# Four engines in a written order: scan and output projection of layer 0 as one software pipeline

## The chip, the cores and the metric

The kernel runs on one core of a Trainium2 chip. A core has five engines that issue independently, each from its own queue in order: TensorE (PE in the profile, its weight loads PEld), VectorE (DVE), ScalarE (ACT), GpSimd (POOL) and SyncE (SP), which here only issues DMAs. The metric is the device time of one execution in microseconds; less is better.

## The reference

Two layers of a hybrid trunk are computed for 128 context tokens and 1024 latent tokens of width 1024. Layer 0 runs windowed attention and a bidirectional state-space scan side by side behind one input projection and adds a joint output projection to the residual. Layer 1 is latent attention. The part that matters is the scan of layer 0, in chunks of 128 tokens for 16 heads of 64, once per direction, and what follows it:

```python
diff = cum[:, :, :, None, :] - cum[:, :, None, :, :]
decay = jnp.exp(jnp.where(causal, diff, -jnp.inf))
scores = jnp.einsum("bclhn,bcshn->bclsh", ch, bh) * decay
y_diag = jnp.einsum("bclsh,bcshp->bclhp", scores, xd)
...
y_off = jnp.einsum("bclhn,bchpn,bclh->bclhp", ch, h_in, jnp.exp(cum))
...
y = y_f + flip(y_b) + d_skip[:, None] * xs
...
s_out = rms_norm(y.reshape(b, L, SSD_INNER) * jax.nn.silu(z), gnorm_w)
return jnp.concatenate([a_out, s_out], axis=-1) @ w_out
...
xl = xl + gate * out
```

The next layer begins with `rms_norm(xl) * (1 + scale) + shift`.

## The kernel before

The work of this stage is cut into nine tiles of 128 tokens: latent tiles 0 to 7 and the context tile, number 8 (`NLT`). Each tile passes two functions.

`scan_out(p, sp, c)` takes the chunk's inputs from DRAM scratch: `BC` (the scan's B and C, transposed), `xs`, `zs` (the SiLU gate), `H` (incoming states, both directions stacked on the partitions). `Gp` is the product of B and C for both head groups (L973), copied to `G` by ScalarE (L975). GpSimd starts `y` with the skip term (L985). For each of two groups of eight heads: two state products on TensorE (`off`, L992), scaled on VectorE (L994) and added into `y` on GpSimd (L995); then two blocks of four heads each. A block loads the cumulated log decays of its heads, broadcast to all partitions, into `cu` (L1000, 512 KB); GpSimd masks each direction (L1003); ScalarE takes the exponentials, eight of 128x128 (L1005); VectorE adds the two directions and multiplies with `G` (L1007, L1008); TensorE multiplies with `xs` into `yacc` (L1011; the profile counts eight instructions for the four products). After both blocks VectorE adds `yacc` to `y` and multiplies with `zs` (L1012, L1013). At the end of the chunk ScalarE squares and sums (L1015), GpSimd computes the reciprocal root (`rstd_of`, L391 and L392), VectorE scales `y` (L1017), TensorE transposes it in two times four steps (L1022), and `split` cuts the result into a high and a low part: a cast on ScalarE (L249) and a subtraction on VectorE (L250).

`project_out` multiplies a tile with the output weights. A product in three parts (`mm3`, L256 to L258) runs over twelve blocks of 128 rows (four from attention, `at`, eight from the scan, `sT`) and two halves of 512 columns, so 72 matmuls of 512 columns per tile. The attention operands come from `project_operands` (a load, and `split`). `residual` multiplies a half with the gate on VectorE (L1060) and adds it to `x` on GpSimd (L1061). Then come a square (L1094), the reciprocal root, a scale (L1096), transposes (L1049), two modulations on VectorE (L1052, L1053) and the store of the next layer's input.

Buffers are rings: `cu`, `zs`, `xs`, `Hc`, `y`, `BC`, `G`, `x` and `rt` have two buffers, `xn` and `nf` one. PSUM has two buffers under each of the tags `pre`, `o`, `tr` and `mm`.

The order within an engine is made by a planner. It runs the program as written against its own model of time and issues on each engine what that model has ready first, earlier lines having priority. The order it finds is fixed when the program is built; on the chip each engine follows its list, and semaphores carry the dependences. `keep_in_program_order` pins an instruction behind the one written before it on its engine; a helper of layer 1, `pinned`, uses it for a few instructions. Chunks 8 and 0 of the scan are written earlier, woven into the stage before (`first_outputs`); the loop then writes, for each tile, the scan of that tile and the projection of the tile before it:

```python
for c in [NLT] + list(range(NLT)) + [None]:
    if c is not None:
        sT = sTs[c] if c in sTs else scan_out(p, op5, c)
    if prev is not None:
        ...
        project_out(p, op5, prev[0], prev[1], gate, start_latents if c is None else None)
```

`start_latents`, called in the middle of the last projection, frees half of the output weights and loads the first weights of layer 1.

Of the kernel before, what the change touches and what calls it, by code (L numbers as in the profile page):

```python
# [214 lines left out]

def bcast_rows(ap, n):
    return ap.unsqueeze(0).broadcast_to([n] + list(ap.shape))
# [3 lines left out]
def hybrid_trunk(ctx: ExitStack, tc: tile.TileContext, I, O, dbg=None, stage=99):  # L221
    nc = tc.nc
    pe, act, dve, pool, dma = nc.tensor, nc.scalar, nc.vector, nc.gpsimd, nc.sync
# [740 lines left out]

    def scan_out(p, sp, c):
        tok = slice(c * 128, (c + 1) * 128)
        BC = p.tile([128, 2, 2, 128], F32, tag="BC", name="BC", bufs=2)
        for d in range(2):
            dma.dma_start(BC[d * 64:(d + 1) * 64, 1], bc_d[1, :, tok].rearrange("(g n) t -> n g t", g=2))
        dma.dma_start(BC[0:64, 0], bc_d[0, :, tok].rearrange("(g n) t -> n g t", g=2))  # L970
        Gp = psum("pre", "Gp")
        for g in range(2):
            pe.matmul(Gp[:, g * 128:(g + 1) * 128], BC[0:64, 0, g], BC[0:64, 1, g], start=True, stop=True)  # L973
        G = p.tile([128, 2, 128], F32, tag="G", name="G", bufs=2)
        act.copy(G, Gp[:, 0:256].rearrange("p (g n) -> p g n", g=2))  # L975
        xs = p.tile([128, D], F32, tag="xs", name="xs", bufs=2)
        dma.dma_start(xs, xs_d[tok])
        zs = p.tile([128, D], F32, tag="zs", name="zs", bufs=2)
        dma.dma_start(zs, z_d[tok])
        if c < NLT:  # L980
            H = p.tile([128, D], F32, tag="Hc", name="Hc", bufs=2)
            dma.dma_start(H[0:64], H_d[c, 0:64])
            dma.dma_start(H[64:128], H_d[NLT - 1 - c, 64:128])
        y = p.tile([128, D], F32, tag="y", name="y", bufs=2)
        pool.tensor_tensor(heads(y), heads(xs), dskip.unsqueeze(2).broadcast_to([128, 16, 64]), ALU.mult)  # L985
        for g in range(2):
            cs = slice(g * 512, (g + 1) * 512)
            if c < NLT:
                for d in range(2):
                    off = psum("pre", "off")  # L990
                    ds = slice(d * 64, (d + 1) * 64)
                    pe.matmul(off, BC[ds, 1, g], H[ds, cs], start=True, stop=True)  # L992
                    t = p.tile([128, 512], F32, tag="rt", name="off", bufs=2)
                    dve.tensor_tensor(heads(t), heads(off), ex[:, d, c * 16 + g * 8:c * 16 + g * 8 + 8].unsqueeze(2).broadcast_to([128, 8, 64]), ALU.mult)  # L994
                    pool.tensor_tensor(y[:, cs], y[:, cs], t, ALU.add)  # L995
            acc = psum("o" if c < NLT else "pre", "yacc")
            for u in range(2):
                h0 = c * 16 + g * 8 + u * 4
                cu = p.tile([128, 4, 2, 128], F32, tag="cu", name="cu", bufs=2)
                dma.dma_start(cu, bcast_rows(cum_d[h0:h0 + 4], 128))  # L1000
                for d in range(2):
                    s = 1 - 2 * d
                    pool.affine_select(cu[:, :, d], cu[:, :, d], [[0, 4], [s, 128]], ALU.is_ge, NEG, base=0, channel_multiplier=-s)  # L1003
                    for j in range(4):
                        act.activation(cu[:, j, d], cu[:, j, d], AF.Exp, bias=nb[:, d, h0 + j:h0 + j + 1])  # L1005
                m = cu[:, :, 0]
                dve.tensor_tensor(m, m, cu[:, :, 1], ALU.add)  # L1007
                dve.tensor_tensor(m, m, G[:, g].unsqueeze(1).broadcast_to([128, 4, 128]), ALU.mult)  # L1008
                for j in range(4):
                    hc = (u * 4 + j) * 64  # L1010
                    pe.matmul(acc[:, hc:hc + 64], m[:, j], xs[:, g * 512 + hc:g * 512 + hc + 64], start=(u == 0 and j == 0), stop=(u == 1 and j == 3))  # L1011
            dve.tensor_tensor(y[:, cs], acc, y[:, cs], ALU.add)  # L1012
            dve.tensor_tensor(y[:, cs], y[:, cs], zs[:, cs], ALU.mult)  # L1013
        ssq = p.tile([128, 1], F32, tag="ssq", name="ssq", bufs=4)
        act.activation(zs, y, AF.Square, accum_out=ssq)  # L1015
        r = rstd_of(p, ssq, D, 1)
        dve.tensor_scalar(y, y, r, None, ALU.mult)  # L1017
        sT = sp.tile([128, 2, KT, 128], F32R, tag="sT", name="sT", bufs=2)
        for q in range(2):
            pt = psum("tr", "pt")  # L1020
            for j in range(4):
                pe.transpose(pt[:, j * 128:(j + 1) * 128], y[:, (q * 4 + j) * 128:(q * 4 + j + 1) * 128], ident)  # L1022
            split(sT[:, 0, q * 4:q * 4 + 4], sT[:, 1, q * 4:q * 4 + 4], pt.rearrange("p (k n) -> p k n", k=4))
        return sT
# [5 lines left out]
    def first_outputs():  # L1030
        for c in (NLT, 0):
            sTs[c] = scan_out(p5, op5, c)
            yield
# [9 lines left out]

    def norm_T(p, l, cond, xh, tok):

        for q in range(2):
            pt = psum("tr", "pt")
            for j in range(4):
                pe.transpose(pt[:, j * 128:(j + 1) * 128], xh[:, (q * 4 + j) * 128:(q * 4 + j + 1) * 128], ident)  # L1049
            full = p.tile([128, 4, 128], F32, tag="nf", name="nf", bufs=1)  # L1050
            bc = lambda v: v[:, l, q * 4:q * 4 + 4, cond].unsqueeze(2).broadcast_to([128, 4, 128])
            dve.tensor_tensor(full, pt.rearrange("p (k n) -> p k n", k=4), bc(scl), ALU.mult)  # L1052
            dve.tensor_tensor(full, full, bc(shift), ALU.add)  # L1053
            dma.dma_start(h1_d[q * 4:q * 4 + 4, :, tok].rearrange("k p n -> p k n"), full)
# [23 lines left out]
    def project_out(p, sp, t, sT, gate, beside=None):  # L1078
        tok = slice(t * 128, (t + 1) * 128)
        at = operands5.pop(t) if t in operands5 else project_operands(p, sp, t)  # L1080
        x = p.tile([128, D], F32, tag="x", name="x", bufs=2)
        dma.dma_start(x, I["x_sample"][0, tok] if t < NLT else I["x_prompt"][0])
        for q in range(2):
            acc = psum("mm", "acc")
            for k in range(12):
                h, l = (at[:, 0, k], at[:, 1, k]) if k < 4 else (sT[:, 0, k - 4], sT[:, 1, k - 4])
                mm3(acc, h, l, *wos[k, q], k == 0, k == 11)
            residual(p, q, acc, x, gate)
            if q == 0 and beside:
                beside()  # L1090
        dma.dma_start(x1_d[tok], x)
        ssq = p.tile([128, 1], F32, tag="ssq", name="ssq", bufs=4)
        xn = p.tile([128, D], F32, tag="xn", name="xn", bufs=1)
        act.activation(xn, x, AF.Square, accum_out=ssq)  # L1094
# [601 lines left out]
```

## Time and profile before

| | |
|---|---|
| median of 3 runs | 1854.38 us (1854.11 to 1855.22) |
| profiled execution | 1849.66 us, its span 1847.8 us |
| busy in the span: PE, PEld | 1713.8 us (93%), 1315.1 us (71%) |
| busy: DVE, ACT, POOL | 1045.4 us (57%), 817.2 us (44%), 744.2 us (40%) |
| mean granted TensorE clock | 0.958 |

Busy time of PE is modelled: a matmul's end includes its way through the array, so rows of matmuls in sequence overlap, and the distance between their starts is what each costs. Rows of time give start, length, engine, line, operation, operands, count and, in brackets, the idle time before it with what ended it. The nine projections of the stage lie between about 704 and 958 us of the span.

### The profile page before, as it was taken

The page shows a single profiled execution, that of the slowest core. Times are in us where ns is not written, and L with a number is a line of the kernel's source. Part 1 is how long each engine was busy: PE and PEld are TensorE (multiplying, and loading weights), DVE is VectorE, ACT ScalarE, POOL GpSimd, SP SyncE. Part 2 cuts the span into 40 slices and gives each one's busy share as a digit, 9 for nine tenths or more (in the row PEclk, how much of TensorE's full clock was granted, in tenths as well). Part 3 has the DMA queues.
Part 4 walks back from the last instruction along what each step waited for, and adds up shares of the span by engine and source line. Part 5 has one row for each costly group of instructions (what it writes and reads, how often), then busy time and mean ns, then how long its engine had stood idle before and what let it go on. Part 6 is the DMA issues. An engine that isn't in the chain of part 4 may idle for free.

```text
span 1847.8 us, 27078 instructions
## 1 busy us (share of the span) xinstructions
PE 1713.8 (93%) x9031; PEld 1315.1 (71%) x9031; DVE 1045.4 (57%) x1989; ACT 817.2 (44%) x1873; POOL 744.2 (40%) x741
## 2 busy tenths in 40 slices
PE   6899999999998878998899999999999998998898
PEld 3799999877775766666688898655665665654486
DVE  4665545655546467777665434655665664564243
ACT  4532323665655354444444322444545544545321
POOL 3510000133343345665623010466666665565432
PEclk9999999999999888999999999899999998999899
DMA  7423423434435697565463532020120121104342
GB/s 260 125 81 93 121 62 111 131 101 132 115 105 146 195 284 240 166 208 159 167 180 85 165 110 79 11 61 23 52 71 23 45 75 28 37 29 122 109 154 91
DMA packets 210655, 210.26 MB, mean 114 GB/s; under 512 B 36162, under 2 KB 175504, under 8 KB 210516
## 3 DMA queue, kind: packets, MB, share of 16 engines
q1 hardware_dynamic: 210372, 208.40, 37.8%
q8 instruction: 72, 1.18, 0.3%
q14 instruction: 67, 0.55, 0.1%
q0 software_dynamic: 144, 0.13, 0.0%
HBM read 151.94 MB, written 51.72 MB: 110 GB/s over the span
## 4 chain that ended last, share of the span: by engine, by line
PE 65%; DMA 11%; DVE 8%; POOL 4%; ACT 3%; issue 3%; SPq 2%; POOLq 0%; DVEq 0%; ACTq 0%
PE acc L256 12%; PE acc L258 12%; PE acc L257 12%; PE acco L1469 6%; PE sc L1448 3%; PE pp L1427 3%; PE sc L1450 3%; PE sc L1449 3%; DMA arenaG<-cum_d 2%; DVE arenaR L250 2%; DMA arenaF<-rd_d 2%; DMA rd_d<-arenaF 2%; PE st L808 1%; DVE arenaF L209 1%; POOL arenaG L1003 1%
## 5 line engine op out<-in xcount | busy, mean ns | idle before, releaser
L256 PE MATMUL acc<-arenaR 128*128 128x384 f32 (+4 forms) x1248 | 426.7, 343 | 20.0 <-ACT arenaR L249 8.0
L1484 POOL TENSOR_TENSOR arenaG<-arenaG 128x512 f32<-128x512 f32 x256 | 332.6, 1318 | 233.8 <-ACT arenaG L1455 201.1
L257 PE MATMUL acc<-arenaR 128*128 128x384 f32 (+3 forms) x1176 | 398.2, 339 | 0.1
L258 PE MATMUL acc<-arenaR 128*128 128x384 f32 (+4 forms) x1152 | 385.9, 336 | 0.2
L256 PEld LDWEIGHTS acc<-arenaR 128*128 128x128 f32 x1248 | 240.0, 193 | 61.7 <-issue 16.0
L1455 ACT ACTIVATE arenaG<-sc 128x512 f32<-128x512 f32 (+1 forms) x304 | 174.7, 580 | 224.2 <-PE sc L1450 206.7
L209 DVE TENSOR_REDUCE arenaF<-pp 128x1 f32<-128x384 f32 (+1 forms) x400 | 198.8, 539 | 102.2 <-PE pp L1427 100.2
L257 PEld LDWEIGHTS acc<-arenaR 128*128 128x128 f32 x1176 | 226.4, 193 | 15.7 <-issue 3.6
L258 PEld LDWEIGHTS acc<-arenaR 128*128 128x128 f32 x1152 | 221.6, 192 | 16.5 <-DVE arenaR L250 2.3
L250 DVE TENSOR_TENSOR arenaR<-arenaF,arenaR 128x512 fp32r<-128x512 f32 (+2 forms) x144 | 133.2, 938 | 73.3 <-ACT arenaR L249 68.5
L249 ACT CAST arenaR<-arenaF 128x512 fp32r<-128x512 f32 (+3 forms) x160 | 101.0, 649 | 138.9 <-issue 22.6
L1469 PE MATMUL acco<-arenaG 128*64 128x512 f32 (+1 forms) x608 | 152.0, 612 | 0.0
L1005 ACT ACTIVATE arenaG<-arenaG,arenaF 128x128 f32<-128x128 f32 x288 | 88.4, 389 | 113.0 <-POOL arenaG L1003 112.7
L1427 PE MATMUL pp<-arenaR 96*128 96x384 f32 (+1 forms) x300 | 97.6, 387 | 12.8 <-DVE arenaF L209 12.5
L749 POOL TENSOR_TENSOR arenaG<-arenaF,arenaG 128x512 fp32r<-128x512 f32 x28 | 47.8, 1708 | 150.8 <-PE acco L753 87.0
L1448 PE MATMUL sc<-arenaR 96*128 96x512 f32 (+1 forms) x228 | 94.9, 416 | 5.6 <-ACT arenaG L1455 5.4
L1427 PEld LDWEIGHTS pp<-arenaR 96*128 96x128 f32 x300 | 58.6, 203 | 57.3 <-DVE arenaF L209 28.4
L1450 PE MATMUL sc<-arenaR 97*128 97x512 f32 (+1 forms) x228 | 90.6, 400 | 1.0 <-DMA arenaR<-arenaF 1.0
L258 PE MATMUL acc<-arenaR,arenaS 128*128 128x512 f32 (+1 forms) x240 | 90.6, 382 | 0.0
L1449 PE MATMUL sc<-arenaR 96*128 96x512 f32 (+1 forms) x228 | 89.9, 394 | 0.0
L1469 PEld LDWEIGHTS acco<-arenaG 128*64 128x64 f32 x608 | 37.3, 141 | 71.4 <-issue 68.3
L1003 POOL TENSOR_SCALAR_AFFINE_SELECT arenaG<-arenaG 128x512 f32<-128x512 f32 x72 | 60.2, 859 | 63.3 <-DMA arenaG<-cum_d 56.4
(328 smaller groups left out, 3331.9 us busy)
## 6 DMA issues: line engine op xcount, KB each, us to landing
arenaF<-in_ada_w_dram SPq DMA_DIRECT2D x96, 256.0 KB
arenaG<-cum_d SPq DMA_DIRECT2D x36, 512.0 KB
arenaF<-in_ab_w_in_dram SPq DMA_DIRECT2D x51, 256.0 KB
z_d<-arenaF SPq DMA_DIRECT2D x36, 128.0 KB
xs_d<-arenaF SPq DMA_DIRECT2D x8, 576.0 KB
arenaF<-xs_d SPq DMA_DIRECT2D x9, 512.0 KB
arenaF<-z_d SPq DMA_DIRECT2D x9, 512.0 KB
x_d<-arenaG SPq DMA_DIRECT2D x9, 512.0 KB
```

The source lines that it names most:

```text
L209: f()
L250: lo_eng.tensor_tensor(lo, src, hi.bitcast(F32), ALU.subtract)
L256: pe.matmul(out, ah, bh, start=first, stop=False)
L257: pe.matmul(out, ah, bl, start=False, stop=False)
L258: pe.matmul(out, al, bh, start=False, stop=last)
L1427: pe.matmul(pp[:, 0:w], AQ[s][0:96, t * 128:(t + 1) * 128], AK[s][0:96, k0:k0 + w], start=True, stop=True)
L1448: pe.matmul(sc[:, 0:n], AK[s][0:96, ks], BQ[s][:, qs], start=True, stop=False)
L1449: pe.matmul(sc[:, 0:n], BK[s][:, ks], AQ[s][0:96, qs], start=False, stop=False)
L1450: pe.matmul(sc[:, 0:n], AK[s][:, ks], AQ[s][:, qs], start=False, stop=True)
L1455: act.activation(pf, sc[:, 0:n], AF.Exp, scale=SCALE_M)
L1469: put = lambda: pe.matmul(acc[0][a * 64:(a + 1) * 64], V[:, a], pfs[a], start=(i < 2 and k < 2), stop=(last and k >= len(todo) - 2))
L1484: pool.tensor_tensor(totals[a], first[a] if i == 1 else totals[a], pfs[a], ALU.add)
```

## The change

`scan_out` and `project_out` are taken apart into methods of two classes, `Scan` and `Project`. The instructions are those of before; each method holds one step: `products` (Gp and its copy), `skip`, `states(g)` (both state products of a group, on TensorE) and `add_states(g)` (scaling and adding them), and for a block of decays `u` the five phases `load_decay`, `causal` (mask), `decay` (exponentials), `weights`, `values`; then `gated(g)`, `square`, `scale` and `turn` (transposes and split). `Project` has `piece(n)`, an eighth of the projection (nine matmuls; pieces 0 to 3 are the first half), `add` (the residual of a half), and `square`, `scale`, `turn(q)`, `modulated(q)`. `cu` gets a third buffer and `zs` loses one. Scans of chunks 8 and 0 call the methods in the old order in the stage before.

The loop is written out anew. In it every instruction of PE, ACT, DVE and POOL is pinned (`Queue.ordered`); the DMAs on SP are not. The loop runs over the tile being projected (`job`); beside it stand the scan of a later chunk (`now`, two ahead of the tile projected), the start of the next scan (`new`), the transposes of the one before (`old`) and the normalisation of the previous projection (`before`).

```diff
+class Queue:
+    ordered = False
...
+    def __getattr__(self, name):
+        f = getattr(self.engine, name)
+        return (lambda *a, **k: self.tc.keep_in_program_order(f(*a, **k))) if Queue.ordered else f
...
-    pe, act, dve, pool, dma = nc.tensor, nc.scalar, nc.vector, nc.gpsimd, nc.sync
+    pe, act, dve, pool = (Queue(tc, e) for e in (nc.tensor, nc.scalar, nc.vector, nc.gpsimd))
+    dma = nc.sync
...
+        def load_z(self):
+            self.zs = self.p.tile([128, D], F32, tag="zs", name="zs", bufs=1)
...
+        def load_decay(self, u):
+            self.cu[u] = self.p.tile([128, 4, 2, 128], F32, tag="cu", name="cu", bufs=3)
...
+        Queue.ordered = True
+        seq = [NLT] + list(range(NLT))
+        new = Scan(p, op5, 1)
+        new.products()
+        new.load_z()
+        for u in range(3):
+            new.load_decay(u)
+        new.causal(0)
+        new.skip()
+        new.states(0)
+        new.decay(0)
+        new.causal(1)
+        new.add_states(0)
+        new.weights(0)
+        new.decay(1)
+        new.causal(2)
+        old = before = None
+        def finish(b):
+            b.square()
+            yield
+            b.scale()
+            b.turn(0)
+            yield
+            b.modulated(0)
+            b.turn(1)
+            yield
+            b.modulated(1)
+        for i, t in enumerate(seq):
+            now, new = new, None
+            if i == NLT:
+                p.drop("xs", "zs", "Hc", "cu", "y", "BC", "G")
+                lp.close()
+            if now and now.c + 1 < NLT:
+                new = Scan(p, op5, now.c + 1)
+            job = Project(p, op5, t)
+            job.piece(0)
+            norm = iter(())
+            if before:
+                before.add(1, gate)
+                norm = finish(before)
+            if i == 1:
+                gate = load_gate(p, 0, 0)
+            if old:
+                old.turn()
+            if now:
+                now.values(0)
+                now.load_decay(3)
+            next(norm, None)
+            if now:
+                now.weights(1)
+                now.decay(2)
+            job.piece(1)
+            next(norm, None)
+            job.piece(2)
+            if now:
+                now.causal(3)
+            next(norm, None)
+            if now:
+                now.values(1)
+                if new:
+                    new.load_decay(0)
+                now.gated(0)
+                now.states(1)
+                now.weights(2)
+                now.decay(3)
+            job.piece(3)
+            next(norm, None)
+            if now:
+                now.add_states(1)
+            job.add(0, gate)
+            if i == NLT:
+                start_latents()
+            job.piece(4)
+            if new:
+                new.causal(0)
+                new.skip()
+            if now:
+                now.values(2)
+                if new:
+                    new.load_decay(1)
+                now.weights(3)
+            if new:
+                new.decay(0)
+            if i < NLT:
+                operands5[seq[i + 1]] = project_operands(p, op5, seq[i + 1])
+            job.piece(5)
+            if new:
+                new.causal(1)
+            if now:
+                now.values(3)
+                if new:
+                    new.load_decay(2)
+                    new.products()
+            job.piece(6)
+            if new:
+                new.states(0)
+            if now:
+                now.gated(1)
+                now.square()
+                if new:
+                    new.load_z()
+                    new.add_states(0)
+                    new.weights(0)
+                    new.decay(1)
+                now.scale()
+            job.piece(7)
+            if new:
+                new.causal(2)
+            old, before = now, job
+        before.add(1, gate)
+        for _ in finish(before):
+            pass
+        Queue.ordered = False
```

More of the change, by code (lines that the diff above doesn't have):

```diff
@@ L213, in flush, with __init__ @@
             self.tick()
+class Queue:
+    ordered = False
+    def __init__(self, tc, engine):
+        self.tc, self.engine = tc, engine
+    def __getattr__(self, name):
+        f = getattr(self.engine, name)
+        return (lambda *a, **k: self.tc.keep_in_program_order(f(*a, **k))) if Queue.ordered else f
 def bcast_rows(ap, n):
@@ L963, in hybrid_trunk @@
     sTs = {}
-    def scan_out(p, sp, c):
[L966 to L971, printed above, removed]
-        for g in range(2):
[L973 to L1024, printed above, removed]
@@ L1026, in hybrid_trunk @@
+    def scan_out(p, sp, c):
+        s = Scan(p, sp, c)
+        s.products()
+        s.load_z()
+        s.skip()
+        for g in range(2):
+            s.states(g)
+            s.add_states(g)
+            for u in (2 * g, 2 * g + 1):
+                for f in (s.load_decay, s.causal, s.decay, s.weights, s.values):
+                    f(u)
+            s.gated(g)
+        s.square()
+        s.scale()
+        s.turn()
     p5 = Space(mem)
@@ L1031, in first_outputs @@
         for c in (NLT, 0):
-            sTs[c] = scan_out(p5, op5, c)
+            scan_out(p5, op5, c)
             yield
@@ L1041, in hybrid_trunk @@
         return
[L1044 to L1054, printed above, removed]
     def residual(p, half, acc, x, gate, adder=pool):
@@ L1136, in hybrid_trunk @@
         gate = load_gate(p, 0, 1)
-        prev = None
-        for c in [NLT] + list(range(NLT)) + [None]:
-            if c is not None:
-                sT = sTs[c] if c in sTs else scan_out(p, op5, c)
-            if prev is not None:
-                if c is None:
-                    p.drop("xs", "zs", "Hc", "cu", "y", "BC", "G")
-                    lp.close()
-                project_out(p, op5, prev[0], prev[1], gate, start_latents if c is None else None)
-                if prev[0] == NLT:
-                    gate = load_gate(p, 0, 0)
-            prev = (c, sT)
+        Queue.ordered = True
```

133 lines of the change are left out of this document (113 added, 20 removed).

## The prediction

> **What bounds the kernel now.** First the page: its chain is TensorE for 65%, with a share of DMA, VectorE and GpSimd that has to come from somewhere.
>
> ```profile
> PE 65%; DMA 11%; DVE 8%; POOL 4%; ACT 3%; issue 3%; SPq 2%; POOLq 0%; DVEq 0%; ACTq 0%
> ```
>
> The changed stage runs from about 704 us, when the first output projection starts, to 958 us. The second view is the table of windows, cut at one repeating point per chunk (first and third window, and the sum of four in a row). Columns: length, then busy us of PE, PEld, DVE, ACT, POOL, granted clock, DMA share, GB/s.
>
> ```profile
> core 0: us, PE busy (x) PEld busy (x) DVE busy (x) ACT busy (x) POOL busy (x), PEclk, DMA share, GB/s
> 784.55:814.65 30.10, 27.39 (x134) 20.75 (x133) 21.63 (x27) 13.83 (x40) 19.10 (x19) 0.94 0.60 190
> 844.71:876.36 31.65, 27.46 (x134) 20.90 (x133) 23.36 (x29) 13.74 (x40) 19.34 (x19) 0.95 0.56 170
> sum 123.22, PE 109.83 PEld 83.28 DVE 89.85 ACT 55.14 POOL 77.09; mean PE 27.46 PEld 20.82 DVE 22.46 ACT 13.79 POOL 19.27
> ```
>
> No engine fills a chunk's 30 us: TensorE has 27.5 by modelled ends, VectorE 22.5, GpSimd 19.3. So I look at the chain of waits (start, length, what) over one chunk, with the same point (second values group) of chunks 2 and 7 as first and last line:
>
> ```profile
> 772.46 1.10 PE yacc L1011 x8
> ...
> 814.65 3.66 DMA arenaG<-cum_d
> 818.45 0.63 POOL arenaG L1003
> 819.11 1.06 ACT arenaG L1005 x4
> ...
> 830.78 2.31 DVE arenaR L250
> 833.09 1.05 DVE arenaG L1008
> 834.18 1.10 PE yacc L1011 x8
> ...
> 924.62 1.10 PE yacc L1011 x8
> ```
>
> Five chunks in 924.62 - 772.46 = 152.2 us: a period of 30.4. The chain runs through the load of the decays (3.66; two buffers), the mask, the exponentials, VectorE, and back to TensorE: a ring of dependences, not one engine.
>
> **TensorE's floor.** Its rows of time (idle before, with releaser, in brackets):
>
> ```profile
> 843.34 0.39 PE L256 MATMUL acc<-arenaR,arenaS 128*128 128x512 f32 x1
> 843.57 1.00 PE L1011 MATMUL yacc<-arenaF,arenaG 128*128 128x64 f32 x8
> 844.38 0.48 PE L257 MATMUL acc<-arenaR,arenaS 128*128 128x512 f32 x1
> ...
> 889.46 1.09 PE L1022 MATMUL pt<-ident,arenaF 128*128 128x128 f32 x8 [1.00 <-DVE arenaF L1017]
> 890.48 1.13 PE L992 MATMUL off<-arenaG,arenaF 64*128 64x512 f32 x4
> ...
> 694.37 1.97 PE L1022 MATMUL pt<-ident,arenaF 128*128 128x128 f32 x8 [2.58 <-DVE arenaF L1017]
> ...
> 936.98 1.00 PE L1011 MATMUL yacc<-arenaF,arenaG 128*128 128x64 f32 x8
> ```
>
> Starts give the pitch: a projection matmul 843.57 - 843.34 = 0.23, a values group 0.81, eight transposes 1.02, the two state products of a group 1.13 when adjacent. A chunk is 72 x 0.23 + 4 x 0.81 + 2 x 1.02 + 2 x 1.13 = 24.1, and Gp at about a pair's half makes 24.7. So up to 5.7 us of each chunk are there to be won; the question is whether the fixed order wins them.
>
> **The change, part by part.**
> Work is not removed. What goes: the wait on the decay load, since a third "cu" buffer lets it be issued after the values group three blocks earlier. What comes: four engines that issue strictly in the written order. So I walk that order, with these rows for VectorE, GpSimd and ScalarE:
>
> ```profile
> 805.27 0.69 DVE L1012 TENSOR_TENSOR arenaF<-yacc,arenaF 128x512 f32<-128x512 f32 x1
> 805.88 0.68 DVE L1052 TENSOR_TENSOR arenaF<-pt,scl 128x512 f32<-128x512 f32 x1
> 810.24 0.69 DVE L1052 TENSOR_TENSOR arenaF<-pt,scl 128x512 f32<-128x512 f32 x1 [1.15 <-DMA h_d<-arenaF]
> 810.96 0.69 DVE L1053 TENSOR_TENSOR arenaF<-arenaF,shift 128x512 f32<-128x512 f32 x1
> 827.15 0.75 DVE L1017 TENSOR_SCALAR arenaF<-arenaF 128x1024 f32<-128x1024 f32 x1 [2.93 <-POOL arenaF L392]
> 829.02 1.76 DVE L1096 TENSOR_SCALAR arenaG<-arenaG,arenaF 128x1024 f32<-128x1024 f32 x1
> 830.70 2.39 DVE L250 TENSOR_TENSOR arenaR<-arenaG,arenaR 128x512 fp32r<-128x512 f32 x1
> 833.01 1.11 DVE L1008 TENSOR_TENSOR arenaG<-arenaG,arenaF 128x512 f32<-128x512 f32 x1
> ```
> ```profile
> 809.58 1.22 POOL L1003 TENSOR_SCALAR_AFFINE_SELECT arenaG<-arenaG 128x512 f32<-128x512 f32 x2 [5.01 <-DMA arenaG<-cum_d]
> 820.08 1.29 POOL L1061 TENSOR_TENSOR arenaG<-arenaG 128x512 f32<-128x512 f32 x1
> 821.34 1.29 POOL L995 TENSOR_TENSOR arenaG<-arenaG 128x512 f32<-128x512 f32 x1
> 826.03 0.46 POOL L391 TENSOR_SCALAR arenaF<-arenaF 128x1 f32<-128x1 f32 x2
> 826.57 1.37 POOL L392 TENSOR_TENSOR arenaF<-arenaF,minus_half 128x1 f32<-128x1 f32 x2
> 830.19 2.35 POOL L985 TENSOR_TENSOR arenaF<-arenaF 128x1024 f32<-128x1024 f32 x1
> ```
> ```profile
> 819.11 2.45 ACT L1005 ACTIVATE arenaG<-arenaG,arenaF 128x128 f32<-128x128 f32 x8 [6.41 <-POOL arenaG L1003]
> 821.47 1.05 ACT L1015 ACTIVATE arenaF<-arenaF 128x1024 f32<-128x1024 f32 x1
> 822.42 0.18 ACT L1015 ACTIVATION_READ_ACCUMULATOR arenaF<-arenaF 128x1 f32 x1
> 826.07 0.60 ACT L249 CAST arenaR<-arenaG 128x512 fp32r<-128x512 f32 x1
> ```
>
> VectorE's pitch is 0.61 between independent operations and 0.72 where one reads the other's output. I add 0.05 to 0.1 for a handover.
>
> The ring, from the end of values(1) of one chunk:
> 1. VectorE must issue gated(0), weights(2), modulated(1) (six operations) before the first product of add_states(1): 4.7.
> 2. GpSimd adds twice into y, then the residual of add(0): 3 x 1.27 and a handover: 8.6.
> 3. Only behind that stands causal(0) of the next chunk; its first half, 0.61: 9.2.
> 4. decay(0), eight exponentials 2.45: 11.7. ScalarE issues the cast of the next projection's operands behind it, 0.60: 12.3.
> 5. VectorE subtracts for that cast. It took 2.39 while GpSimd's 2.35 us product ran, and an operation beside the mask took 1.11; by then skip is about done and causal(1) runs, so I take 1.1: 13.5. **This is the added wait that costs most**: gated(1), add_states(0), weights(0) and scale are queued behind it on VectorE, though values(3) has been over since 9.1 (states 1.1, three pieces of 2.07, two values groups on TensorE).
> 6. gated(1) and the first product of add_states(0): 2.0, 15.5; two adds on GpSimd 2.6, 18.1; rstd, half of 0.46 + 1.37, 0.9, 19.0; scale between 0.75 and 1.76, 1.2 taken since the next mask runs beside it: 20.3. TensorE, which issued pieces 6, 7 and 0 and the small products by 17, stands idle for turn for 3.3 us; this pays out part of the win.
> 7. add(1): 0.7 on VectorE, 1.4 on GpSimd, square 1.3 (with its read), rstd 1.0, scale of the previous job 0.8: 25.5. TensorE, through with turn, values(0) and piece 1 by 24.3, waits again.
> 8. Four transposes 0.5, piece 2 2.1, four transposes 0.5, values(1) 0.8, and the tail of its last matmul 0.2: 29.6.
>
> **Clock.** After the idle 2.58 us at 694.37 eight transposes took 1.97, after 1.00 us 1.09. With 3.3 us idle I take the slow figure; the second cast of turn then ends 0.4 later than the residual add does, and the ring becomes 30.0. The Trainium skill ("TensorE: Matmul & The Clock Gate", Part 1) says an idle window of about 3.4 us halves the clock for about as long; an estimate by it costs piece 1 as well and gives 30.2.
>
> **Costs hidden.** Loads stay on SP's queue, unpinned. A decay load lands in 3.66: for causal(0) it is issued after values(1) and needed 8.6 later; for causal(1) after values(2), with about 2 us to spare; for causal(3) and causal(2) 4 and more. With "zs" single, z waits for square at 16.2 and is read a chunk later. The x1 store and the h1 stores are issued in the order of their producers; the gate's second load waits for add(1) of the context job and has 20 us. Each costs 0, and 1 to 2 us a chunk if SP's order puts a late store ahead of a mask's load. In the last job the splits that start_latents issues stand ahead of the last add(1) on ScalarE and VectorE; their weights can be loaded early, and eight of each at 0.6 to 1.1 fit under pieces 4 to 7 (8.3): 0, or a few us once if a load is late. Keeping two state products adjacent saves TensorE 1 us a chunk, which is off the ring: 0.
>
> **Head and tail.** Pinned VectorE starts behind the last weight split, and the last projection's accumulator is read at 957.9:
>
> ```profile
> 711.25 0.74 DVE L253 SCALAR_TENSOR_TENSOR arenaR<-arenaF,vecs,arenaR 128x512 fp32r<-128x512 f32 x1
> ...
> L1060 DVE TENSOR_TENSOR arenaG<-acc,arenaF x18: 678/691/692, 719.9 to 957.9; 128x512 f32<-128x512 f32 x18
> ```
>
> Head: 712.0, two state products and two weights operations 2.6, values(0) 0.9, pieces 1 and 2 4.2, values(1) 0.9 give 720.6; the rest of chunk 0 is woven in, so 722 (719 to 728). Six rings follow to chunk 7, then 9.1 to its values(3). Tail: before, 957.9 - 938.0 = 20 us remained there. Now two whole projections and two pieces remain: 2 x 16.6 + 4.1, turn 1.0, four half turns 2.0, and two waits for the previous job's scale, 1.6 and 0.8: 43. So the order pulls the scans forward by about 20 us and pays it back behind them.
>
> **Sum.** 722 + 6 x 30.0 + 9.1 + 43 = 954.1 against 957.9: -3.8. The profiled run took 1849.66 (span 1847.8 and 1.9 around it) and would take 1845.9; it lies 4.7 under the median of 1854.38, so against the median 1850.6. Break-even is a ring of 30.6.
>
> **Bounds of the ring.** Low: subtract 0.68, scale 0.75, no slow clock, 28.7: -12. High: subtract 2.39, scale 1.76, the mask's first half doubled as DVE and POOL collide, 32.5: +11. The head adds -3 to +6.
>
> **Rivals.**
> - *Slower, 0.30.* VectorE's operations on two SBUF operands, and the scale, stretch while GpSimd runs (1.76 against 0.75, 2.39 against 0.68). Packed closer, they meet on the ring: subtract +1.3 and scale +0.6 give 31.9, +7.6 us, 1862. It decides from +0.6 per ring. For it: 829.02 and 830.70 in every chunk. Against: on this ring the two engines mostly take turns. The Trainium skill ("GPSIMD Engine Reference", Key points) states the shared interface for just these forms; the rows agree.
> - *Loads order, no change, 0.08.* SP's planned order holds a mask's load behind a store; the period stays at 30.4: 956.5, -1.4, 1853.
> - *Faster, towards TensorE's floor, 0.20.* If a step of the ring isn't one (the cast early enough, the waits before turn covered), it loses 1.5 to 4 us; at the floor of 24.7 plus a dozen changes of operand at 0.1 it is 26: -28, 1827, and half way there -15, 1839. For it: 5.7 us of slack in every chunk. Against: the written order, which the engines can't leave.
>
> **How the numbers follow.** A measurement of this kernel can tell about 0.2%, 3.7 us, from no change. Forecast case 0.42 (ring 28.7 to 30.6): its middle sits on that line, so 0.23 lies beyond and 0.19 within. Faster 0.23 + 0.20 = 0.43; same 0.19 + 0.08 = 0.27; slower 0.30. The case's own range is 1843 to 1855; the whole range takes in the slower rival and the faster one half way, and leaves a tenth on each side: 1837 to 1866.
>
> **What would show it.** In the trace after: the decay load gone from the chain; a period near 30.0 between second values groups; ScalarE's operand cast right behind decay(0) and gated(1) right behind its subtract, 4 us after values(3); TensorE idle some 3 us before turn and 1 us before the half turn; about 43 us from chunk 7's last values group to the last residual. I'm wrong if gated(1) follows values(3) at once, or if the two-operand operations run over 1.5 us on the ring.

## The result, and the profile after

The changed kernel takes 1905.74 us (median of 4, 1898.72 to 1908.0), against 1854.8 us for the kernel before (4 runs): a ratio of 1.0268, 95% interval 1.0241 to 1.0295. Forecast were 1850.6 us and a range of 1837 to 1866. The profiled execution took 1906.34 us, its span 1904.6; granted clock 0.944, before 0.958. Times and ratios here and below are of fast runs: one execution of e3 (1924.0 us), two of e15 (2320.6 and 4072.9) and one of before (5567.9) were slow and are left out.

The chain line of the page, as shown of before, says little now: it adds up to 48% of the span, since the chain breaks off inside the pinned stage.

```profile
PE 34%; DMA 6%; DVE 4%; ACT 2%; SPq 1%; issue 1%; POOL 0%; DVEq 0%; POOLq 0%; ACTq 0%
```

The windows answer the same question as before, cut from gated(0) of one chunk to that of the next (columns as in the prediction):

```profile
core 0: us, PE busy (x) PEld busy (x) DVE busy (x) ACT busy (x) POOL busy (x), PEclk, DMA share, GB/s
761.30:798.12 36.82, 28.86 (x134) 22.05 (x135) 21.76 (x28) 14.57 (x44) 18.55 (x19) 0.91 0.51 157
...
837.28:875.87 38.59, 29.53 (x134) 22.27 (x134) 21.86 (x27) 13.65 (x40) 18.55 (x19) 0.87 0.50 146
...
sum 153.20, PE 116.93 PEld 89.51 DVE 86.33 ACT 55.30 POOL 74.10; mean PE 29.23 PEld 22.38 DVE 21.58 ACT 13.82 POOL 18.53
```

A chunk now takes 153.20 / 4 = 38.3 us where it took 123.22 / 4 = 30.8. VectorE, ScalarE and GpSimd are busy as long as before (21.6, 13.8, 18.5 against 22.5, 13.8, 19.3): the loss is waiting. Every pinned instruction carries line L226 (the lambda of `Queue`), so rows are told apart by engine, tile and shape. First GpSimd, from the timeline of one chunk:

```profile
873.17 1.67 POOL L226 TENSOR_SCALAR_AFFINE_SELECT arenaG<-arenaG 128x512 f32<-128x512 f32 x2 [2.26 <-DMA arenaG<-cum_d]
883.30 1.22 POOL L226 TENSOR_SCALAR_AFFINE_SELECT arenaG<-arenaG 128x512 f32<-128x512 f32 x2 [8.46 <-DMA arenaG<-cum_d]
884.49 1.90 POOL L226 TENSOR_TENSOR arenaF<-arenaF 128x1024 f32<-128x1024 f32 x1
886.35 2.60 POOL L226 TENSOR_TENSOR arenaF<-arenaF,arenaG 128x512 f32<-128x512 f32 x2
888.92 1.71 POOL L226 TENSOR_TENSOR arenaG<-arenaG 128x512 f32<-128x512 f32 x1
```

The order written was: two adds into y, the residual of add(0), then causal(0) and skip of the next chunk. Here the mask (883.30) and skip (884.49, 1024 wide) stand ahead of the adds (886.35) and the residual (888.92), and GpSimd sits idle 8.46 us until the mask's load lands. GpSimd did not keep the written order. Not all of the idle time is loss, since the adds need VectorE's first product, which starts at 880.57: here they start 5.78 us behind that, and 0.77 us in the run that keeps the written order (e1 below: 864.99, 865.76). So about 5 us a chunk are lost, 2 of them to the load and 3 to the mask and skip that stand in front. The rows of VectorE, TensorE and SyncE's queue show who pays:

```profile
875.86 0.32 SPq L1030 DMA_DIRECT2D arenaG<-cum_d  x1
...
880.57 1.28 DVE L226 TENSOR_TENSOR arenaG<-off,arenaF 128x512 f32<-128x512 f32 x2
...
887.65 0.69 DVE L226 TENSOR_TENSOR arenaG<-acc,arenaF 128x512 f32<-128x512 f32 x1 [5.80 <-POOL arenaF L226]
...
891.27 1.94 PE L226 MATMUL yacc<-arenaF,arenaG 128*128 128x64 f32 x8 [7.10 <-issue]
893.14 1.22 PE L226 MATMUL Gp<-arenaF 64*128 64x128 f32 x4
894.29 3.91 PE L226 MATMUL acc<-arenaR,arenaS 128*128 128x512 f32 x9
...
898.13 1.13 PE L226 MATMUL off<-arenaG,arenaF 64*128 64x512 f32 x4
899.29 1.29 DVE L226 TENSOR_TENSOR arenaG<-off,arenaF 128x512 f32<-128x512 f32 x2 [4.55 <-PE off L226]
```

VectorE makes the products of add_states(1) (880.57), then waits 5.80 us: add(0) needs an `rt` buffer that GpSimd's late adds still read. weights(3) stands behind add(0), so TensorE idles 7.10 us before values(3), and runs the next piece in 3.91 us at a low clock (2.33 at full clock, the piece at 876.82). The load was issued at 875.86, right behind values(1) as the third buffer allows, and the mask starts 7.4 us later; in the chain of before a load took 3.66.

By the prediction's own sum, up to the last read of the projection's accumulator (rows of after; the bound before was 957.87):

```profile
726.57 1.00 PE L226 MATMUL yacc<-arenaF,arenaG 128*128 128x64 f32 x8
...
950.75 1.00 PE L226 MATMUL yacc<-arenaF,arenaG 128*128 128x64 f32 x8
...
962.83 1.94 PE L226 MATMUL yacc<-arenaF,arenaG 128*128 128x64 f32 x8 [2.73 <-issue]
...
1013.43 0.68 DVE L226 TENSOR_TENSOR arenaG<-acc,arenaF 128x512 f32<-128x512 f32 x1
```

These are values(1) of chunks 1 and 7, values(3) of chunk 7, and the last residual.

| term | predicted | measured | difference |
|---|---|---|---|
| head, values(1) of chunk 1 ends | 722 | 727.6 | +5.6 |
| six rings | 6 x 30.0 | 6 x 37.36 = 224.2 | +44.2 |
| values(1) to values(3), chunk 7 | 9.1 | 13.0 | +3.9 |
| tail | 43 | 48.6 | +5.6 |
| last residual | 954.1 | 1013.4 | +59.3 |

### The profile page after: what moved, and what is told of

The parts are those of the page before. It is cut to its first block, busy times and chain, and to the rows that moved or that the text cites. A ratio compares the mean times of both kernels' runs of the same rounds, so it can differ in the third digit from the quotient of the medians.

```text
span 1904.6 us, 27072 instructions
## 1 busy us (share of the span) xinstructions
PE 1731.4 (91%) x9031; PEld 1326.2 (70%) x9031; DVE 1038.8 (55%) x1989; ACT 816.9 (43%) x1873; POOL 738.5 (39%) x741
## 5 line engine op out<-in xcount | busy, mean ns | idle before, releaser
L270 PE MATMUL acc<-arenaR 128*128 128x384 f32 (+4 forms) x1176 | 397.0, 338 | 19.8 <-ACT arenaR L263 8.2
L271 PE MATMUL acc<-arenaR 128*128 128x384 f32 (+3 forms) x1104 | 369.5, 335 | 0.1
L272 PE MATMUL acc<-arenaR 128*128 128x384 f32 (+4 forms) x1080 | 358.5, 333 | 0.8 <-DVE arenaR L226 0.6
L270 PEld LDWEIGHTS acc<-arenaR 128*128 128x128 f32 x1176 | 226.4, 193 | 53.5 <-issue 12.4
L271 PEld LDWEIGHTS acc<-arenaR 128*128 128x128 f32 x1104 | 212.1, 192 | 12.8 <-issue 3.1
L272 PEld LDWEIGHTS acc<-arenaR 128*128 128x128 f32 x1080 | 208.4, 193 | 13.5 <-issue 2.5
L264 DVE TENSOR_TENSOR arenaR<-arenaF,arenaR 128x512 fp32r<-128x512 f32 (+2 forms) x137 | 124.4, 920 | 71.3 <-ACT arenaR L263 64.0
L263 ACT CAST arenaR<-arenaF 128x512 fp32r<-128x512 f32 (+3 forms) x153 | 96.6, 650 | 120.1 <-issue 22.4
L226 PE MATMUL acc<-arenaR,arenaS 128*128 128x512 f32 x432 | 122.7, 433 | 0.0
L226 PEld LDWEIGHTS acc<-arenaR,arenaS 128*128 128x128 f32 x432 | 87.9, 210 | 30.5 <-issue 11.5
L1609 PEld LDWEIGHTS pp<-arenaR 96*128 96x128 f32 x300 | 59.3, 206 | 60.8 <-DVE arenaF L209 31.0
L226 ACT ACTIVATE arenaG<-arenaG,arenaF 128x128 f32<-128x128 f32 x224 | 68.2, 388 | 52.2 <-POOL arenaG L226 52.2
```

Of the source, the lines that this page charges most:

```text
L226: return (lambda *a, **k: self.tc.keep_in_program_order(f(*a, **k))) if Queue.ordered else f
L270: pe.matmul(out, ah, bh, start=first, stop=False)
L271: pe.matmul(out, ah, bl, start=False, stop=False)
L272: pe.matmul(out, al, bh, start=False, stop=last)
L1609: pe.matmul(pp[:, 0:w], AQ[s][0:96, t * 128:(t + 1) * 128], AK[s][0:96, k0:k0 + w], start=True, stop=True)
```

## The experiments

All at a glance. Ring: us per chunk, from gated(0) of chunk 2 to that of chunk 6, a quarter (of before, the four windows of the prediction). Last residual: us in the profiled execution. Ratio: to runs of the kernel before on the same chip (medians 1849.6 to 1854.8), with its 95% interval. Where no ring is given, scans of two chunks overlap and no point repeats.

| kernel | ring | last residual | us | ratio |
|---|---|---|---|---|
| before | 30.8 | 957.9 | 1854.8 | 1 |
| after | 38.3 | 1013.4 | 1905.7 | 1.0268 (1.0241 to 1.0295) |
| e1_chain | 33.8 | 991.1 | 1874.0 | 1.0142 (1.0100 to 1.0183) |
| e2_hoist | 38.6 | 1019.7 | 1905.7 | 1.0298 (1.0271 to 1.0325) |
| e3_nopin | | 952.2 | 1837.2 | 0.9933 (0.9907 to 0.9958) |
| e4_buffers | | 961.9 | 1848.0 | 0.9993 (0.9970 to 1.0016) |
| e5_cast | 34.1 | 995.2 | 1887.8 | 1.0216 (1.0186 to 1.0245) |
| e6_free_pe | 37.4 | 1014.4 | 1913.2 | 1.0341 (1.0314 to 1.0368) |
| e7_free_pool | 33.4 | 992.8 | 1872.1 | 1.0127 (1.0098 to 1.0156) |
| e8_free_dve | 30.8 | 969.7 | 1855.4 | 1.0022 (0.9997 to 1.0047) |
| e9_weights3 | 32.4 | 986.0 | 1866.3 | 1.0084 (1.0056 to 1.0111) |
| e10_weights | 33.3 | 986.6 | 1869.5 | 1.0106 (1.0074 to 1.0137) |
| e11_states | 33.0 | 984.8 | 1866.8 | 1.0081 (1.0054 to 1.0107) |
| e12_pe_act | 31.9 | 976.3 | 1867.1 | 1.0075 (1.0046 to 1.0104) |
| e13_three | 30.5 | 973.4 | 1857.5 | 1.0040 (1.0015 to 1.0065) |
| e14_three_tail | 30.5 | 970.8 | 1852.5 | 1.0013 (0.9995 to 1.0031) |
| e15_nopin_again | | 949.1 | 1836.7 | 0.9926 (0.9906 to 0.9945) |
| e16_three_nopin | | 947.4 | 1832.1 | 0.9899 (0.9882 to 0.9916) |

A caution on the last columns. What follows the last residual is planned anew for each kernel and takes from 876 us (e9, 1862.2 - 986.0) to 891 (after, 1904.6 - 1013.4); one and the same program in two rounds gave 881.2 and 885.3 (e3, e15). Nor does the ring begin at one time: in the pinned kernels gated(0) of chunk 1 starts between 726.7 us (e6) and 734.9 (e14). Differences of under 15 us between kernels are therefore read from the ring.

**1. GpSimd's order (e1, e2).** In the built program a mask is two instructions, a register move and the mask. `keep_in_program_order` ties an instruction to the one written just before it on its engine; for a mask that is its own move, and the move is tied to nothing. One row of the trace after shows the moves, one for each of the 56 pinned masks:

```profile
L226 POOLq MOVE  x56: 29/29/29, 702.7 to 949.7; - x56
```

e1 ties each pinned instruction to the last pinned one as well:

```diff
+        def put(*a, **k):
+            ins = self.tc.keep_in_program_order(f(*a, **k))
+            if self.last:
+                self.tc.add_manual_dep(ins.ins, self.last, ..., reason="order")
+            self.last = ins.ins.name
```

> Theory A (the mask is issued with a register move in front of it, is pinned to that move only, and so escapes from GpSimd's written order: causal(0) and skip stand ahead of the two y adds and the residual add, and wait there for the decay load). This kernel adds the missing edge from each pinned instruction to the pinned one before it, so that GpSimd's order is the written one. A: the stretch from values(1) to the scale falls from 29.3 to about 20 us, the period from 37.4 to 29-31, the time to 1845-1860. Theory B (VectorE and GpSimd collide on SBUF operands in the packed order): period over 35, time over 1890. Theory C (decay loads are late with three buffers, wherever the mask stands): period 33-36, time 1870-1890.

e2 is e1 with the order that the trace of after shows written out by hand:

```diff
+            if new:
+                new.causal(0)
+                new.skip()
             if now:
                 now.add_states(1)
             job.add(0, gate)
...
+                    new.causal(2)
                     new.add_states(0)
```

> As the kernel with the missing edges, but causal(0) and skip are written ahead of add_states(1) and add(0), and causal(2) ahead of add_states(0): GpSimd's order in the changed kernel, this time on purpose. A: that order alone makes the loss, so 1898-1912, period 37 +-1. B and C: the order of masks and adds matters little, so the time is that of the kernel with the missing edges, within 8 us.

e2 brought back the whole loss (1905.74, ring 38.6), with the same wait in GpSimd's rows:

```profile
889.30 1.23 POOL L230 TENSOR_SCALAR_AFFINE_SELECT arenaG<-arenaG 128x512 f32<-128x512 f32 x2 [7.96 <-DMA arenaG<-cum_d]
890.49 1.90 POOL L230 TENSOR_TENSOR arenaF<-arenaF 128x1024 f32<-128x1024 f32 x1
892.35 2.60 POOL L230 TENSOR_TENSOR arenaF<-arenaF,arenaG 128x512 f32<-128x512 f32 x2
```

So the hoisted masks are worth 1905.7 - 1874.0 = 32 us, shown from both sides. Of these, 22 lie ahead of the last residual (1013.4 - 991.1; 29 from e2, 1019.7 - 991.1) and the rest behind the stage. GpSimd's idle time ahead of its masks falls with them; groups of after and of e1:

```profile
L226 POOL TENSOR_SCALAR_AFFINE_SELECT arenaG<-arenaG 128x512 f32<-128x512 f32 x56 | 42.8, 787 | 98.4 <-DMA arenaG<-cum_d 83.1 <-PE yacc L226 6.4 <-PE acc L226 6.3
```
```profile
L230 POOL TENSOR_SCALAR_AFFINE_SELECT arenaG<-arenaG 128x512 f32<-128x512 f32 x56 | 43.5, 800 | 23.4 <-DMA arenaG<-cum_d 15.6 <-PE yacc L230 5.2 <-PE yacc L1064 2.6
```

But e1 missed its expectation: the ring is 33.8 us, not 29 to 31. The order as it was written, kept, is still slower than before: the last residual stands 33 us behind that of before (991.1, 957.9). Ring and time fall into the ranges of theory C, late loads. Yet the only loads that GpSimd still waits for in e1's ring are those of causal(3), 2.1 to 3.3 us a chunk, and decay(3) behind that mask ends at 860.81, 6.9 us before weights(3) starts; e13 below comes to 30.5 with the same three buffers.

**2. The pin and the buffers (e3, e4).** e3 drops one line, e4 gives the kernel before only the new buffers:

```diff
-        Queue.ordered = True
```
```diff
-        zs = p.tile([128, D], F32, tag="zs", name="zs", bufs=2)
+        zs = p.tile([128, D], F32, tag="zs", name="zs", bufs=1)
-                cu = p.tile([128, 4, 2, 128], F32, tag="cu", name="cu", bufs=2)
+                cu = p.tile([128, 4, 2, 128], F32, tag="cu", name="cu", bufs=3)
```

> The new program text and the new buffers, but nothing pinned: the planner orders all engines, with the written order only as priority. A: no engine is held to a sequence that GpSimd doesn't follow, so most of the loss goes: 1845-1870. Rival (the written order is bad on TensorE, VectorE and ScalarE, whoever keeps it): 1885-1910.

> The kernel before with only the rings changed: three buffers for the decays, one for z. A: the decay load (3.66 us in the old chain) leaves the ring, up to 6 x 3.66 = 22 us faster, at worst no change: 1833-1856. Theory C (with three buffers the loads collide and land late): 1860-1880.

The buffers alone change nothing that can be measured; GpSimd's masks wait 48.6 us for loads in e4's stage and 49.3 in that of before, so with the planner's order the third buffer did not take the load off the chain. The new loop without pins is 0.7% faster than before; of that gain 6 us lie in the stage (952.2, 957.9) and the rest behind it. All of the loss, and more, is the pins.

**3. Which engine's written order (e5 to e8, e12).** e5 moves the operands' cast to behind add(0), where its subtract stands ahead of weights(3) on VectorE. e6, e7 and e8 are e1 with one engine left to the planner, e12 with two:

```diff
             job.add(0, gate)
+            if i < NLT:
+                operands5[seq[i + 1]] = project_operands(p, op5, seq[i + 1])
...
             if new:
                 new.decay(0)
-            if i < NLT:
-                operands5[seq[i + 1]] = project_operands(p, op5, seq[i + 1])
```
```diff
-        if not Queue.ordered:
+        if not Queue.ordered or self.engine is self.tc.nc.vector:
```

> The chained written order (1874, ring 33.4) with one move: the cast and subtract of the next projection's operands stand ahead of the exponentials of decay(0) instead of behind them. Theory of step 5 (the subtract is the added wait that costs most): gated(1) comes about 3 us earlier in each chunk, ring 30.4 or less, 1852 to 1860. Theory from the trace of the chained kernel (the products of add_states(0), behind gated(1), wait for TensorE's late and slow state products anyway): under 1 us per ring, 1867 to 1876.

> The chained written order on VectorE, GpSimd and ScalarE; TensorE alone is left to the planner. If TensorE's written order is what remains (it stands before values(3) and turn while projection pieces are ready, then runs at a low clock): ring about 31, 1850 to 1860. If the ring through VectorE and GpSimd is what remains: 1868 to 1876.

> The chained written order on TensorE, VectorE and ScalarE; GpSimd alone is left to the planner. If the written place of causal(0) behind three adds of y and the residual (step 3) is what remains: 1845 to 1862. If an early mask at the head of GpSimd's queue, waiting for its load, is what costs whenever it stands there: 1890 to 1910, as in the changed kernel. No matter: 1868 to 1880.

> The chained written order on TensorE, GpSimd and ScalarE; VectorE alone is left to the planner. If VectorE's written queue (add(0) and the subtract ahead of gated(1) and the products) is what remains: ring 30 to 31.5, 1850 to 1862. If it isn't: 1866 to 1878.

VectorE is the one: left free, the ring is 30.8 and the time that of before. Its rows in e8 show what the planner does with it: weights(3) ahead of add(0), the subtract between the two halves of weights(0), weights(1) ahead of scale.

```profile
858.29 0.68 DVE L1055 TENSOR_TENSOR arenaG<-arenaG 128x512 f32<-128x512 f32 x1
...
861.29 1.17 DVE L1056 TENSOR_TENSOR arenaG<-arenaG,arenaF 128x512 f32<-128x512 f32 x1
862.38 0.68 DVE L1126 TENSOR_TENSOR arenaG<-acc,arenaF 128x512 f32<-128x512 f32 x1
865.22 0.69 DVE L1068 TENSOR_TENSOR arenaF<-yacc,arenaF 128x512 f32<-128x512 f32 x1 [2.16 <-PE yacc L230]
...
868.88 1.11 DVE L273 TENSOR_TENSOR arenaR<-arenaG,arenaR 128x512 fp32r<-128x512 f32 x1
```

gated(1) (865.22) no longer stands behind the subtract. GpSimd free gives no change (ring 33.4), although the planner, too, puts causal(0) ahead of the adds, and GpSimd waits 60.1 us for loads in the stage, against 15.6 in e1. Its rows in e7:

```profile
872.03 1.23 POOL L1045 TENSOR_SCALAR_AFFINE_SELECT arenaG<-arenaG 128x512 f32<-128x512 f32 x2 [8.16 <-DMA arenaG<-cum_d]
873.23 2.65 POOL L1034 TENSOR_TENSOR arenaF<-arenaF,arenaG 128x512 f32<-128x512 f32 x2
```

Here the mask starts 3.9 us after its load was issued (868.09), and the adds start 1.14 us behind VectorE's product (872.09). So the mask's place at the head of the queue cost time in after, where its load was late, and none here. In after, the load of x and a store go out 1.5 and 1.1 us ahead of it (874.34, 874.77, 875.86), in e7 5.7 and 3.5 us (862.39, 864.61, 868.09); that these make the load late is likely, not shown.

TensorE free is 39 us worse, which no theory expected: in its rows it runs the projection's pieces early and then stands idle before values(3) with none left (1.69 and 3.21 us). e5 was expected to gain or to change nothing, and lost 14 us. Of the 12.3 us between its profiled span and e1's, 4 lie ahead of the last residual (the ring lost 0.3) and 8 behind the stage. The 4 are there before the ring begins (gated(0) of chunk 1 at 732.5, in e1 at 727.9), so on the ring the move changed nothing, as its second theory has it; why the rest grew is open. With VectorE and GpSimd both free:

> The chained written order on TensorE and ScalarE alone; VectorE and GpSimd both left to the planner. If VectorE's queue is all that the written order costs: 1850 to 1858, as with VectorE alone left free. If TensorE's written order alone is what still stands between that and the kernel without any pin (1837.6): the same 1850 to 1858. If GpSimd's pin adds to VectorE's: 1838 to 1848.

The ring is 31.9, worse than with VectorE alone free: freedom of two engines does not add up, and none of the three outcomes expected came out. What the planner did worse there stays open.

**4. Which waits in VectorE's order (e9 to e11).** In e1, two rows of VectorE and three of TensorE carry the ring:

```profile
870.72 1.93 PE L230 MATMUL yacc<-arenaF,arenaG 128*128 128x64 f32 x8 [2.04 <-issue]
...
873.73 4.09 PE L230 MATMUL acc<-arenaR,arenaS 128*128 128x512 f32 x9
...
874.14 1.16 DVE L230 TENSOR_TENSOR arenaR<-arenaG,arenaR 128x512 fp32r<-128x512 f32 x1 [3.52 <-ACT arenaR L230]
...
877.76 1.13 PE L230 MATMUL off<-arenaG,arenaF 64*128 64x512 f32 x4
...
878.92 1.29 DVE L230 TENSOR_TENSOR arenaG<-off,arenaF 128x512 f32<-128x512 f32 x2 [2.29 <-PE off L230]
```

There are two waits in a row on VectorE: 3.52 us for ScalarE's cast (step 5), then 2.29 us for TensorE's state products, which stand behind a late values(3) and a piece at a low clock. e9 puts weights(3) ahead of add(0); e10 also weights(2) ahead of gated(0) and weights(1) ahead of scale; e11 puts states(0) ahead of piece(6).

```diff
                 now.add_states(1)
+                now.weights(3)
             job.add(0, gate)
...
-                now.weights(3)
```
```diff
+            if new:
+                new.states(0)
             job.piece(6)
-            if new:
-                new.states(0)
```

> The chained written order (1874, ring 33.4) with one move on VectorE: weights(3) ahead of add(0). If TensorE's late values(3) and cold piece 6 alone hold the ring: values(3) comes 2 us earlier, the state products 3 to 4 us earlier, the products of add_states(0) start behind gated(1) without their 2.3 us wait, 1858 to 1864. If the later add(0) hands its 2 us through the residual, causal(0), decay(0), cast and subtract to gated(1): 1868 to 1876.

> The chained written order with the places that the planner gave the weights on VectorE in the run that left VectorE free (1855, ring 30.7), written by hand: weights(2) ahead of gated(0), weights(3) ahead of add(0), weights(1) ahead of scale. If the place of these operations in VectorE's written queue is what was left of the loss: 1850 to 1862, ring 30.5 to 31.5. If it is the planner's finer freedom (between the two operations of a weights group, around the subtract): 1864 to 1874.

> The chained written order with one move on TensorE: the state products of states(0) ahead of piece(6) instead of behind it. VectorE's products of add_states(0) waited 2.3 us for them in each chunk. If that wait lies on the ring: ring 31, 1857 to 1865. If another wait takes its place (the sum of GpSimd's adds, rstd, scale): 1868 to 1876.

Each single move lies between its two expectations: 1.4 us per ring for e9, 0.8 for e11. The wait for TensorE is gone, and the subtract stands alone on the ring; VectorE's rows in e9:

```profile
876.34 1.16 DVE L230 TENSOR_TENSOR arenaR<-arenaG,arenaR 128x512 fp32r<-128x512 f32 x1 [4.95 <-ACT arenaR L230]
877.42 0.68 DVE L230 TENSOR_TENSOR arenaF<-yacc,arenaF 128x512 f32<-128x512 f32 x1
878.13 0.69 DVE L230 TENSOR_TENSOR arenaF<-arenaF 128x512 f32<-128x512 f32 x1
878.74 1.28 DVE L230 TENSOR_TENSOR arenaG<-off,arenaF 128x512 f32<-128x512 f32 x2
```

All three places of the weights by hand (e10) gave no more than the one: ring 33.3 and 1869.5 us, the second of the outcomes expected. The places alone are not what VectorE's freedom is worth.

**5. The moves together (e13 to e16).** e13 is e1 with weights(3), states(0) and the cast moved; e14 ends the pin at the last job; e15 is e3 again; e16 is e13 without `Queue.ordered = True`. In e13 the cast stands behind weights(3) and add(0), so that it delays neither. The edit of e14 to e13:

```diff
             if i == NLT:
+                Queue.ordered = False
```

> The chained written order (1874, ring 33.7) with three moves together: weights(3) ahead of add(0), the state products of states(0) ahead of piece(6), and the cast and subtract of the next operands ahead of decay(0). Theory (two waits in a row: first TensorE's late state products, behind them step 5's subtract): with the first gone the subtract's place is worth 2.5 to 4 us per ring, ring 29 to 30.5, 1844 to 1854. Rival (the three moves only repeat one another, GpSimd's adds and masks set the ring at 32.4 as with weights(3) alone): 1862 to 1870.

> As the kernel with the three moves, and the order is pinned only up to the last job: what follows the eight scans' loop is left to the planner. If the pin costs the tail what the trace shows over the run with VectorE free (48 against 42.7 us from the last gated(1) to the last residual): 4 to 7 us less than with the three moves alone. If the tail is TensorE's work alone: the same within 2 us.

> The change without its pins, once more on another chip beside the others: 1833 to 1843, ratio to the kernel before 0.990 to 0.996, if the gain of the code's new order of emission is real; 1846 to 1854 if the first look was the luck of its chip.

> The change without its pins and with the three moves in the order of emission. If the planner's own costs set the order and the emission only breaks ties: 1833 to 1843, as without the moves. If the moves help it too: 1822 to 1832.

The ring falls to 30.5, from 32.4 (e9) and 33.0 (e11): the waits were in series. weights(3) and states(0) were not run together without the cast, so how much of the last 1.9 us is the cast's own is not separated; alone (e5) it gained nothing. In e13 gated(1) follows values(3) at once, and GpSimd is next on the ring: VectorE waits 3.46 us for its adds and the reciprocal root, which stand behind causal(1).

```profile
865.38 0.69 DVE L230 TENSOR_TENSOR arenaF<-yacc,arenaF 128x512 f32<-128x512 f32 x1
...
875.56 1.11 DVE L230 TENSOR_SCALAR arenaF<-arenaF 128x1024 f32<-128x1024 f32 x1 [3.46 <-POOL arenaF L230]
```

The time fell short of its expectation (1857.5 for 1844 to 1854). e14's tail, from the last gated(1) to the last residual, is 43.3 us against 46.3 in e13; the times (1852.5, 1857.5) have intervals that overlap. Without pins the gain over before came back in a second round (e15); its expectation speaks of another chip, but by the results both rounds ran on chip 1, so a gain of this chip alone is not excluded. e16 is the fastest kernel here: 1832.11 us, 1.0% under before. Its advantage over e15 is not resolved, since their intervals overlap (0.9882 to 0.9916, 0.9906 to 0.9945).

## Why the prediction was wrong

**The step that failed first** is step 3, "Only behind that stands causal(0)", and with it "the written order, which the engines can't leave". The walk took the text of the loop for GpSimd's queue. The mask slipped its pin, stood at the head of the queue, and waited for a load that step 3 would have covered. This was worth 32 us of the 51 in the whole time (e1, e2). In the stage alone it was the smaller part: of the 55.5 us by which the last residual came later than before, 22 are the masks' and 33 are left in e1, whose order is the written one. By the terms of the sum e1 has 727.8, 6 x 33.4, 13.4 and a tail of 49.3: 991.1 against 954.1.

**"Loads hidden, cost 0, or 1 to 2 us a chunk"** held only with that cover. The same load that step 3 gives 8.6 us takes 7.4 in after, next to the other loads and stores of its chunk; with causal(0) in its written place (e1), GpSimd waits 15.6 us for loads in the whole stage, not 83.1. For causal(3) the working had "4 and more"; in e1 GpSimd is ready for it 2.3 us after the load's issue (889.51, 887.18) and waits 2.13 us, off the ring.

**Step 5**, the subtract as "the added wait that costs most", is the step that failed next. In after it did not act at all: the subtract is done 1.1 us before gated(1), which follows values(3) (to 893.21) at once, as the prediction's sign of being wrong has it.

```profile
891.10 1.11 DVE L226 TENSOR_TENSOR arenaR<-arenaG,arenaR 128x512 fp32r<-128x512 f32 x1
...
893.32 0.69 DVE L226 TENSOR_TENSOR arenaF<-yacc,arenaF 128x512 f32<-128x512 f32 x1 [1.11 <-PE yacc L226]
```

In e1 it was a real wait (3.52 us) but not the last one to end. The walk had values(3) "over since 9.1"; measured are 12.4 us behind values(1) in e1 (860.29 to 872.65), and in after 17.4 (875.83 to 893.21; 13.0 in chunk 7, which has no next chunk's mask). It had left out that weights(3) stands behind add(0) on VectorE, beside GpSimd's adds: 1.28 and 1.63 us where the walk had 0.61 and 0.72. TensorE then ran cold. By the walk's own marks e1 is 1.5 us late at the end of the subtract (15.0 for 13.5) and 4.5 at the ends of scale (24.8 for 20.3) and of values(1) (34.1 for 29.6); 2.29 of the 3 us between are the wait for the state products. Step 5 decided only where the state products were early (e9: 4.95 us ahead of the subtract). That both head and tail came 6 us late is not explained; with the pin off in the last job the tail is 43.3 (e14).

**The slower rival** had collisions of VectorE and GpSimd at +1.9 per ring, on the subtract and the scale. These two stretched no further than the walk had them (1.16 and 1.11 us in e1, 1.1 and 1.2 in the walk); the operations of weights did, past the 1.5 us that the prediction named as a sign of being wrong (1.63). That is one part of e1's 33.8, above the high bound of 32.5; the ring of after comes from a mechanism that was in no case. The Trainium skill ("GPSIMD Engine Reference", Key points) says that the two engines contend when VectorE reads two operands from SBUF; the rows of weights agree (0.69 us with GpSimd idle, at 861.67, and 1.28 and 1.63 beside its adds, at 867.67 and 868.99, in e1).

**Right** were the last part of the ring (scale to the end of values(1): 29.6 - 20.3 = 9.3 us in the walk, 9.3 in after and e1) and that a low clock would come, though at another place: before turn TensorE idled 1.98 us in e1, not 3.3, and the eight transposes took 1.09, not 1.97; cold were values(3) and the piece behind it. Two near hits are luck: the ring of 30.5 in e13 against 30.0, since the walk's ring runs through the subtract and e13's through GpSimd's adds, and the tail of 42.7 in e8 against 43, in a kernel with VectorE free. In the range, the case that was missing is an order other than the written one.

## What to carry to other kernels

Before walking a written order, read it off the built program or the trace: an instruction that the compiler gives a companion (a register move) can slip an order made of neighbours, and at the head of a strict queue it holds up everything behind it. Idle time ahead of an instruction is not yet its price: what counts is when the work behind it could have started (e7). In a ring, fix the waits from the one that ends last backwards: a real wait is worth nothing while a later one covers it, so single moves understate what they do together (1.4 and 0.8 us off the ring alone, 3.3 for the three). The same code wholly left to the planner was faster in both comparisons here (e3 against e1, e16 against e13).

## What the runs showed of the hardware

GpSimd's queue passes nothing: it stood idle 8.46 us at a mask whose load was on its way, with skip behind it, whose input had been loaded from 854.25 on, and for the last 2 us with an add behind it that could have run. The Trainium skill ("TensorE: Matmul & The Clock Gate", the table at its head) calls the queues of VectorE, ScalarE and GpSimd strictly first in, first out; the trace agrees.

TensorE fell to the low clock after idle times that are short, and their length alone does not set it. In e1, after 2.04 us, values took 1.93 us and the next piece 4.09 (2.33 at full clock), and the granted clock of three windows in four is 0.90; but after 1.98 us ahead of turn the eight transposes took 1.09, as at full clock. In e13 three windows of four have 1.00, with waits of up to 1.64 us; in the remaining one (0.89) two state products took 2.07 us after 0.86 us of idle time (805.99), where the same pair in the next window took 1.12 after 0.85 (837.43).

```profile
860.34:894.47 34.13, 28.91 (x134) 22.07 (x135) 22.23 (x28) 13.90 (x42) 18.55 (x19) 0.90 0.57 166
```
```profile
855.80:886.01 30.21, 26.50 (x134) 19.96 (x134) 20.58 (x27) 13.65 (x41) 19.00 (x19) 1.00 0.59 187
```

The Trainium skill ("TensorE: Matmul & The Clock Gate", Part 1) puts the change to half clock after at least one idle window of about 3.4 us; here shorter idle times were enough, and the measurement decides. What sets the clock in these cases is not shown by any run here.
